# A one-core decoder layer in split float32: the first four weight chunks loaded by pairs of k tiles on one queue

## The chip, the cores and the metric

The kernel runs on one core of a Trainium2 chip. The engines are TensorE (PE, matrix products into PSUM), VectorE (DVE), ScalarE (ACT), GpSimd (POOL) and SyncE (SP, which here only issues DMAs). ACT can issue DMAs on a queue of its own. The metric is the time of one execution in microseconds (us) on the device. Three runs of the kernel before gave 439.91, 440.33 and 441.61 us; the median is 440.33.

## The reference

One decoder layer on 256 tokens of width 1024, in float32:

```
h = rmsnorm(x, norm1_g)
u = h @ w_in                      # columns: x_rnn | g_rnn | q | k | v | branch gates
ya = rg_lru(causal_dwconv(x_rnn)) * gelu(g_rnn)      # recurrent branch
yb = attention(rmsnorm(q), rmsnorm(k), v)            # 8 heads of 128, causal, one block of 256
merged = sigmoid(ga) * (ya @ w_proj_rnn) + sigmoid(gb) * (yb @ w_proj_attn)
x = x + merged @ w_out
h = rmsnorm(x, norm2_g)
x = x + (gelu(causal_dwconv(h @ w_up)) * (h @ w_gate)) @ w_down
```

The norm's division is applied after the product with w_in: the kernel multiplies x by the gains norm1_g alone, and brings in 1/rms later, on the products.

## The kernel before, in words

**Products in three parts.** To keep float32's precision at a higher rate, each operand is split into hi (rounded to the reduced type float32r) and lo (the rest). A product is three matmuls, hi by hi, hi by lo and lo by hi (`mm3`, lines 292 to 295). So each weight chunk that is loaded as `raw` goes through a cast to `hi` on ACT (or on DVE for a few) and a subtraction to `lo` on DVE (`split_part`, lines 274 to 276).

**The stream.** The weights are a list of chunks of up to 1 MB (128 partitions by 2048 elements) in the order of use, loaded on SP's queue into three `raw` buffers and split into four `hi` and three `lo` buffers. A pool of 23 half buffers (128 by 1024) holds activations. `advance(i)` makes all splits up to chunk i and keeps some loads ahead. The table `AFTER` (line 37) lists, by hand, after which quarter of which unit of PE work an item (a split `s4`, a step `stats`, `bcast`, `evac3`) is put into the program.

**Who sets the order.** The program is traced once, and a planner then decides the order of instructions on each engine: it goes by program order as priority, and by when its own table of costs says that an instruction is ready. An instruction that is ready earlier may go ahead. Inside `tc.manual_schedule` ACT and DVE keep the written order. Semaphores are put in by the framework. On the chip, each engine works through its queue in order. At most a fixed number of DMAs is under way before an issuing queue waits for an earlier one.

**The start (lines 334 to 408).** The first stage, rx, is the product of x with the first four chunks (256 columns each, 1024 rows in 8 k tiles of 128). A loop over k tiles works on all four chunks side by side in four PSUM banks (lines 706 to 710). While the first data come, nine matmuls on a tile of ones (`WARM`, line 31; lines 340 to 342) keep PE busy. Loads are cut into pieces of 1, 1, 2, 2 and 2 k tiles (`pieces`, line 345). For each piece, SP issues the load of transposed x (`xT`, line 356), and then the four chunks' pieces (line 359); for the first two pieces, chunks 2 and 3 are issued by ACT. Rows are 1 KB in those pieces and 2 KB in the rest. `pv` (line 336), all the small vectors in one tile of 170 columns, norm1_g's among them, is ACT's first load. x in token order (`xs`) comes behind the fourth piece's weights.

Then (lines 398 to 408, in the written order) each piece's x is scaled and split into `xgh` on ACT and `xgl` on DVE, and each chunk's piece is split into `hi` and `lo`; for the very first, DVE does the cast.

**Behind it.** rg takes the next four chunks. `norm1_stats` (line 416) squares `xs` on ACT, a chain of small DVE operations makes 1/rms and the diagonal tiles `dg`, and in rg's third quarter PE spreads them to all partitions (`rbcp`, line 429). Only then are rx's and rg's sums multiplied and moved out of PSUM. `gqk` (line 537) is the product of two gain columns of `pv`, used to scale k; `make_decay` on POOL also reads `pv`.

Of the kernel before, what the change touches and what calls it, by code (L numbers as in the profile page):

```python
# [8 lines left out]
F32 = mybir.dt.float32  # L9
# [6 lines left out]
P = 128  # L16
# [14 lines left out]
HALVES, SMALLS, WARM, RAWS = 23, 10, 9, 3  # L31
# [133 lines left out]
def trunk_layer(ctx: ExitStack, tc: tile.TileContext, xT, x, vec, win_fm, win_tm, wri, wpr, wpa,  # L165
# [17 lines left out]
    def f(ap):  # L183
        return ap.bitcast(F32)
# [21 lines left out]
    class Wide:  # L206


        def __init__(self, name, dt=F32):
            self.h = [half(f"{name}{i}", dt) for i in range(2)]  # L210

        def __getitem__(self, at):
            s = at[1]
            i = s.start // 1024
            assert (s.stop - 1) // 1024 == i
            return self.h[i][:, s.start - i * 1024:s.stop - i * 1024]
# [118 lines left out]
    pv = const.tile([P, V_N], F32, name="pv")  # L335
    nc.scalar.dma_start(pv, vec)
# [8 lines left out]
    pieces = [(0, 1), (1, 2), (2, 4), (4, 6), (6, 8)]  # L345
    START = 4
    for i in range(START):
        if i < 2:
            raw[i] = wp.tile([P, 2048], F32, tag="raw", name=f"raw{i}")
            split_tiles()  # L350
        else:
            raw[i], hi[i], lo[i] = Wide(f"raw{i}"), Wide(f"hi{i}", F32R), Wide(f"lo{i}", F32R)
    ptr["load"] = ptr["split"] = START
    xs = const.tile([P, 2, D], F32, name="xs")
    for a, b in pieces:
        nc.sync.dma_start(kt(xTs.half(a // 4))[:, a % 4:a % 4 + b - a, :], xT[:, a:b, :])
        for i in range(START):
            s = slice(a * 256, b * 256)
            (nc.scalar if b <= 2 and i >= 2 else nc.sync).dma_start(raw[i][:, s], stream[i][:, s])
        if a == 0:  # L360
            nc.scalar.preload_act_table(AF.Exp)
        if a == 4:
            for t in range(2):
                nc.sync.dma_start(xs[:, t, :], x[t * P:(t + 1) * P, :])
# [34 lines left out]
    with tc.manual_schedule(engines={mybir.EngineType.Activation, mybir.EngineType.DVE}):  # L399
        for a, b in pieces:  # L400
            for k in range(a, b):
                g = pv[:, V_G1 + k:V_G1 + k + 1]
                nc.scalar.activation(xgh[k], xTs[k], AF.Copy, scale=g)  # L403
                if a == 0:
                    split_part(0, slice(a * 256, b * 256), True)
                nc.vector.scalar_tensor_tensor(xgl[k], xTs[k], g, f(xgh[k]), op0=OP.mult, op1=OP.subtract)
            for i in range(a == 0, START):
                split_part(i, slice(a * 256, b * 256))
# [627 lines left out]
```

## Time and profile before

| | |
|---|---|
| median of 3 runs | 440.33 us (439.91 to 441.61) |
| profiled execution | 440.18 us, its span 438.4 us |
| PE busy | 431.3 us, 98% of the span |
| DVE, ACT, POOL busy | 325.1, 248.5, 45.8 us |
| data moved | 95.89 MB, mean 219 GB/s |

All times inside the profile count from the span's start. A row of the page or of a list of groups names the line of the kernel, the engine, the operation and what it writes and reads. In an order-of-time row, the first two numbers are the start and the time covered; square brackets give the idle time before and what ended it. "xN" is a count. PEld is the weight load into PE, which overlaps the products; PE's ends are modelled, so starts are the safer numbers. The waits list has total, times and longest, in us. Idle time of an engine that isn't the bottleneck costs nothing.

### The profile page before, as it was taken

Reading aid. Unit: us, or ns where it says so; the run is one execution under the profiler, and the core shown is the slowest. Engines: PE = TensorE matmul, PEld = TensorE weight load, DVE = VectorE, ACT = ScalarE, POOL = GpSimd, SP = SyncE. Lnnn points to the kernel's source line nnn. Section 1 sums busy time; section 2 is a strip of 40 time slices with the busy share of each in tenths; the row PEclk is TensorE's granted clock in tenths of the full one; section 3 lists DMA queues with packets and bytes.
Section 4 is the critical chain, followed back from the end, with each engine's and each line's share of the span. In section 5 each row is a group of like instructions: output and inputs, shape, how many; then the busy total and the mean of one; then the engine's idle time right before and its main releaser. Section 6 shows DMA issues by size and latency. Waiting matters only on the chain.

```text
span 438.4 us, 5841 instructions
## 1 busy us (share of the span) xinstructions
PE 431.3 (98%) x2224; PEld 368.4 (84%) x2224; DVE 325.1 (74%) x448; ACT 248.5 (57%) x294; POOL 45.8 (10%) x99
## 2 busy tenths in 40 slices
PE   8999999999899999999999999999999999999996
PEld 8999988887788888888888888888888888888985
DVE  4689869768789999765576796576776779965943
ACT  4596748682888999944232373345437257352910
POOL 2038306424240000000000000000000000000000
PEclk9999999999999999999999999999999999999999
DMA  7987652857877754554553555877995494897202
GB/s 218 387 310 256 229 193 62 240 227 233 301 253 238 230 184 151 183 171 171 191 193 96 193 191 155 280 284 275 321 309 187 148 395 190 293 340 288 86 1 96
DMA packets 30268, 95.89 MB, mean 219 GB/s; under 512 B 2848, under 2 KB 12448, under 8 KB 26144
## 3 DMA queue, kind: packets, MB, share of 16 engines
q1 hardware_dynamic: 29520, 94.91, 62.0%
q10 hardware_dynamic: 720, 0.61, 0.6%
q8 instruction: 17, 0.28, 0.3%
q14 instruction: 11, 0.09, 0.1%
HBM read 87.12 MB, written 8.39 MB: 218 GB/s over the span
## 4 chain that ended last, share of the span: by engine, by line
PE 87%; DVE 5%; POOL 3%; DMA 2%; issue 1%; ACT 1%; SPq 0%; DVEq 0%
PE acc L293 4%; PE acc L294 4%; PE acc L295 4%; PE up L293 4%; PE up L294 4%; PE gt L293 4%; PE gt L294 4%; PE up L295 4%; PE gt L295 4%; POOL rsq L388 2%; DMA raw<-in_win_fm 2%; PE rg L295 2%; PE rg L294 2%; PE rg L293 2%; PE gb L293 2%; PE v L294 2%
## 5 line engine op out<-in xcount | busy, mean ns | idle before, releaser
L276 DVE TENSOR_TENSOR lo<-raw,hi 128x2048 fp32r<-128x2048 f32 (+3 forms) x92 | 170.9, 1868 | 40.1 <-ACT hi L275 8.5
L275 ACT CAST hi<-raw 128x2048 fp32r<-128x2048 f32 (+3 forms) x88 | 137.6, 1576 | 90.7 <-PE pa L295 16.0
L294 PE MATMUL up<-lo,h2h 128*128 128x512 f32 x80 | 31.2, 391 | 0.0
L294 PE MATMUL gt<-lo,h2h 128*128 128x512 f32 x80 | 31.1, 389 | 0.0
L294 PE MATMUL acc<-lo,fah 128*128 128x512 f32 x80 | 31.1, 389 | 0.0
L293 PE MATMUL acc<-hi,fah 128*128 128x512 f32 x80 | 31.1, 389 | 0.0
L295 PE MATMUL up<-hi,h2l 128*128 128x512 f32 x80 | 31.0, 389 | 0.0
L295 PE MATMUL gt<-hi,h2l 128*128 128x512 f32 x80 | 31.0, 389 | 0.0
L293 PE MATMUL up<-hi,h2h 128*128 128x512 f32 x80 | 30.9, 392 | 0.0
L293 PE MATMUL gt<-hi,h2h 128*128 128x512 f32 x80 | 30.8, 389 | 0.0
L295 PE MATMUL acc<-hi,fal 128*128 128x512 f32 x80 | 30.5, 389 | 0.0
L853 ACT ACTIVATE fc<-fu,pv 128x256 f32<-128x256 f32 x20 | 10.4, 590 | 19.8 <-DVE fu L865 19.8
L293 PE MATMUL rx<-xgh,hi 128*128 128x256 f32 x64 | 18.3, 288 | 0.8 <-ACT xgh L403 0.8
L295 PE MATMUL rx<-xgh,lo 128*128 128x256 f32 x64 | 18.2, 284 | 0.2 <-DVE lo L276 0.2
L293 PE MATMUL rg<-xgh,hi 128*128 128x256 f32 x64 | 18.2, 284 | 0.0
L294 PE MATMUL rx<-xgl,hi 128*128 128x256 f32 x64 | 18.2, 284 | 0.0
L295 PE MATMUL rg<-xgh,lo 128*128 128x256 f32 x64 | 18.1, 283 | 0.0
L294 PE MATMUL rg<-xgl,hi 128*128 128x256 f32 x64 | 18.1, 283 | 0.0
L293 PEld LDWEIGHTS up<-hi,h2h 128*128 128x128 f32 x80 | 15.0, 188 | 3.3 <-ACT h2h L794 0.2
L293 PEld LDWEIGHTS gt<-hi,h2h 128*128 128x128 f32 x80 | 15.0, 188 | 3.2
L295 PEld LDWEIGHTS gt<-hi,h2l 128*128 128x128 f32 x80 | 15.0, 188 | 3.2
L295 PEld LDWEIGHTS acc<-hi,fal 128*128 128x128 f32 x80 | 15.0, 188 | 3.1
(251 smaller groups left out, 1078.5 us busy)
## 6 DMA issues: line engine op xcount, KB each, us to landing
raw<-in_win_tm SPq DMA_DIRECT2D x12, 1024.0 KB, 5.2
raw<-in_win_fm SPq DMA_DIRECT2D x11, 1024.0 KB, 5.7
raw<-in_wup SPq DMA_DIRECT2D x11, 1024.0 KB, 5.7
raw<-in_wgate SPq DMA_DIRECT2D x11, 1024.0 KB, 5.7
raw<-in_wdown SPq DMA_DIRECT2D x11, 1024.0 KB, 6.0
raw<-in_wpr SPq DMA_DIRECT2D x4, 1024.0 KB, 5.0
raw<-in_wpa SPq DMA_DIRECT2D x4, 1024.0 KB, 4.9
raw<-in_wout SPq DMA_DIRECT2D x4, 1024.0 KB, 4.8
```

Of the source, the lines that this page charges most:

```text
L275: (nc.vector.tensor_copy if on_dve else nc.scalar.copy)(hi[i][:, s], raw[i][:, s])
L276: nc.vector.tensor_sub(lo[i][:, s], raw[i][:, s], f(hi[i][:, s]))
L293: nc.tensor.matmul(o, ah, bh, start=start, stop=False, skip_group_check=skip)
L294: nc.tensor.matmul(o, ah, bl, start=False, stop=False, skip_group_check=skip)
L295: nc.tensor.matmul(o, al, bh, start=False, stop=stop, skip_group_check=skip)
L388: nc.gpsimd.tensor_tensor(z, y, y, op=OP.mult)
L853: nc.scalar.activation(c, u, AF.Identity, scale=w(2), bias=pv[:, V_FB + m:V_FB + m + 1])
```

## The change

- The four first chunks are no longer four tiles with pieces by k; they are pieces by pair of k tiles (a = 0 to 3) and pair of chunks (c = 0, 1), each 128 by 1024 elements, laid out as chunk, k tile, column. Pieces of a = 0 and 1 lie in `raw`, `hi` and `lo` buffers, two pieces to a buffer, those of a = 2 and 3 in half buffers. `Column` gives the matmuls the view of one chunk.
- All their loads are on SP's queue, in the order of use: x of two k tiles, then the two pieces. Every row is 2 KB. In the first pair, the piece of chunks 0 and 1 is loaded as two transfers, one a chunk.
- ACT's queue issues only `g1`, the eight columns of norm1_g. `pv`, then `xs`, are loaded on SP's queue behind all the weights of rx.
- Eight warming matmuls instead of nine.
- The splits follow the pieces: in the first, DVE casts chunk 0's two k tiles one at a time; later pieces are cast on ACT and subtracted on DVE as 128 by 1024 (the second chunk's first pair as 128 by 512).
- rx's matmuls go by pairs of k tiles: for each pair and chunk, both k tiles of the first half of its columns, then both of the second.
- `gqk` is made on POOL in two operations, so that DVE's queue doesn't hold a reader of `pv` early.
- What follows rx's first unit (`stats s4`) is queued behind the last hand-ordered instruction of ACT and of DVE (`tc.issue_after`).

```diff
-HALVES, SMALLS, WARM, RAWS = 23, 10, 9, 3
+HALVES, SMALLS, WARM, RAWS = 23, 10, 8, 3
...
-    class Wide:
+    class Column:
+        def __init__(self, pieces, i):
+            self.pieces, self.i = pieces, i
         def __getitem__(self, at):
+            k, c = divmod(at[1].start, 256)
+            return self.pieces[k // 2, self.i // 2][:, self.i % 2, k % 2, c:c + at[1].stop - at[1].start]
...
-    pv = const.tile([P, V_N], F32, name="pv")
-    nc.scalar.dma_start(pv, vec)
+    g1 = const.tile([P, KT], F32, name="g1")
+    nc.scalar.dma_start(g1, vec[:, V_G1:V_G1 + KT])
...
-    pieces = [(0, 1), (1, 2), (2, 4), (4, 6), (6, 8)]
+    def pieces(name, dt=F32):
+        p = {}
+        for a in range(2):
+            t = wp.tile([P, 2048], dt, tag=name, name=f"{name}s{a}", bufs={"raw": RAWS, "hi": 4, "lo": 3}[name])
+            for c in range(2):
+                p[a, c], p[a + 2, c] = t[:, c * 1024:(c + 1) * 1024], half(f"{name}s{a + 2}{c}", dt)
+        return {k: v.rearrange("p (c k n) -> p c k n", c=2, k=2) for k, v in p.items()}
...
-    for a, b in pieces:
+    def load_x(a, b):
         nc.sync.dma_start(kt(xTs.half(a // 4))[:, a % 4:a % 4 + b - a, :], xT[:, a:b, :])
-        for i in range(START):
-            s = slice(a * 256, b * 256)
-            (nc.scalar if b <= 2 and i >= 2 else nc.sync).dma_start(raw[i][:, s], stream[i][:, s])
...
+    def load_w(a, c, js=slice(0, 2)):
+        nc.sync.dma_start(sraw[a, c][:, js].rearrange("p c k n -> p c (k n)"),
+                          win_fm[2 * c + js.start:2 * c + js.stop, :, a * 512:(a + 1) * 512].rearrange("c p n -> p c n"))
...
+    load_x(0, 2)
+    load_w(0, 0, one)
+    nc.scalar.preload_act_table(AF.Exp)
+    load_w(0, 0, two_)
+    load_w(0, 1)
+    for a in range(1, 4):
+        load_x(2 * a, 2 * a + 2)
+        for c in range(2):
+            load_w(a, c)
+    pv = const.tile([P, V_N], F32, name="pv")
+    nc.sync.dma_start(pv, vec)
+    for t in range(2):
+        nc.sync.dma_start(xs[:, t, :], x[t * P:(t + 1) * P, :])
...
+        def split_x(k):
+            g = g1[:, k:k + 1]
+            nc.scalar.activation(xgh[k], xTs[k], AF.Copy, scale=g)
+            return lambda: nc.vector.scalar_tensor_tensor(xgl[k], xTs[k], g, f(xgh[k]), op0=OP.mult, op1=OP.subtract)
+
+        def split_w(a, c, js=slice(0, 2), ks=slice(0, 2), e=nc.scalar.copy):
+            r, h, l = sraw[a, c][:, js, ks], shi[a, c][:, js, ks], slo[a, c][:, js, ks]
+            start_end[0] = e(h, r).ins
+            return lambda: start_end.__setitem__(1, nc.vector.tensor_sub(l, r, f(h)).ins)
+
+        x = split_x(0)
+        w = split_w(0, 0, one, one, nc.vector.tensor_copy)
+        x()
+        w()
+        w = split_w(0, 0, one, two_, nc.vector.tensor_copy)
+        x = split_x(1)
+        x()
+        w()
+        split_w(0, 0, two_)()
+        split_w(0, 1)()
+        for a in range(1, 4):
+            for k in (2 * a, 2 * a + 1):
+                split_x(k)()
+            for c in range(2):
+                split_w(a, c)()
...
-    nc.vector.scalar_tensor_tensor(gqk, pv[:, V_QG:V_QG + 1], SC, pv[:, V_KG:V_KG + 1], op0=OP.mult, op1=OP.mult)
+    nc.gpsimd.tensor_scalar(gqk, pv[:, V_QG:V_QG + 1], SC, None, op0=OP.mult)
+    nc.gpsimd.tensor_tensor(gqk, gqk, pv[:, V_KG:V_KG + 1], op=OP.mult)
...
-            for k in range(KT):
+            for a in range(KT // 2):
                 for n in range(START):
-                    fm_mm(rx_ps[n], n, xgh, xgl, (k,), True)
+                    fm_mm(rx_ps[n], n, xgh, xgl, (2 * a, 2 * a + 1), True)
...
-            for n in AFTER.get(f"{name}.{q}", "").split():
-                advance(int(n[1:])) if n[1:].isdigit() and n[0] == "s" else item[n]()
+            with tc.issue_after(start_end[0]) if name == "rx0" else nullcontext(), \
+                    tc.issue_after(start_end[1]) if name == "rx0" else nullcontext():
+                for n in AFTER.get(f"{name}.{q}", "").split():
+                    advance(int(n[1:])) if n[1:].isdigit() and n[0] == "s" else item[n]()
```

31 lines of the change are left out of this document (5 added, 26 removed).

## The prediction

> **What bounds the kernel now.** I read the page first, then the waits of TensorE (PE), then busy time by stage, then the first microseconds in order of time.
>
> ```profile
> span 438.4 us, 5841 instructions
> PE 431.3 (98%) x2224; PEld 368.4 (84%) x2224; DVE 325.1 (74%) x448; ACT 248.5 (57%) x294; POOL 45.8 (10%) x99
> PE 87%; DVE 5%; POOL 3%; DMA 2%; issue 1%; ACT 1%; SPq 0%; DVEq 0%
> ```
>
> PE is busy for 98% of the span and holds 87% of the chain that ended last. An edit helps only where PE stands still. The list of what PE waited for is short:
>
> ```profile
> PE v L293 <- ACT hi L275: 0.9, 1, 0.9
> PE rx L293 <- ACT xgh L403: 0.8, 1, 0.8
> PE v L294 <- DVE lo L276: 0.5, 1, 0.5
> PE rx L295 <- DVE lo L276: 0.2, 1, 0.2
> ```
>
> Two of these lie in rx, the stage the change rewrites; the two in v come far behind it and the change does not name them. The stage view gives the size of the start. Its columns are window, length, then busy time and count for PE, weight loads, DVE, ACT, POOL, then the granted clock, DMA share and GB/s.
>
> ```profile
> 0.00:5.42 5.42, 3.62 (x18) 3.43 (x19) 1.09 (x5) 1.84 (x3) 2.24 (x12) 1.00 0.64 189
> 5.42:29.52 24.10, 23.88 (x192) 23.36 (x193) 16.35 (x35) 16.66 (x34) 0.48 (x2) 1.00 0.96 340
> 29.52:53.00 23.48, 23.48 (x198) 23.48 (x197) 20.15 (x28) 15.74 (x13) 15.91 (x34) 1.00 0.71 260
> 34.01 0.45 PE rbcp L429 x4
> ```
>
> rx starts at 5.42 and rg at 29.52. The rg stage has 192 products of the same shape and the rbcp matmuls in 23.48 us: (23.48 - 0.45) / 192 = 0.12 us each. So rx, also 192, needs 23.03 us and took 24.10: it lost 1.07 us to late operands. With the wait for the first operands, all that the change can win directly is 5.42 + 1.07 = 6.5 us less whatever the first load and splits still need. Now the first load:
>
> ```profile
> 0.72 0.37 SPq L356 DMA_DIRECT2D xT<-in_xT  x1
> 1.16 0.93 ACTq L359 DMA_DIRECT2D raw<-in_win_fm  x2
> 2.12 1.28 ACT L361 ACT_TABLE_LOAD   x1 [2.12 <-issue]
> 3.82 0.99 ACTq L359 DMA_DIRECT2D raw<-in_win_fm  x2
> 4.48 0.32 DVE L275 CAST hi<-raw 128x256 fp32r<-128x256 f32 x1 [0.31 <-DMA raw<-in_win_fm]
> 4.83 0.42 DVE L276 TENSOR_TENSOR lo<-raw,hi 128x256 fp32r<-128x256 f32 x1
> 4.86 0.51 ACT L403 ACTIVATE xgh<-xT,pv 128x256 fp32r<-128x256 f32 x1 [1.46 <-DMA raw<-in_win_fm]
> 5.40 0.48 DVE L406 SCALAR_TENSOR_TENSOR xgl<-xT,pv,xgh 128x256 fp32r<-128x256 f32 x1
> 5.42 0.69 PE L293 MATMUL rx<-xgh,hi 128*128 128x256 f32 x2 [0.76 <-ACT xgh L403]
> 5.80 1.09 DVE L276 TENSOR_TENSOR lo<-raw,hi 128x256 fp32r<-128x256 f32 x3
> ```
>
> The weights landed in time for DVE's cast at 4.48, but xgh, the scaled x, began only at 4.86: ACT was issuing two more weight DMAs from 3.82 to 4.81. PE's first product waited for xgh until 5.42.
>
> **The change part by part.**
>
> *ACT's queue.* Four weight DMAs and pv leave it; a load of g1 (4 KB in rows of 32 B) stays. ACT's 3.82 to 4.81 is gone, so xgh is bound by x and g1. Landing times from the tile views, x first, weights second, and pv's from the DMA view:
>
> ```profile
> DMA to landing us min/median/max: 3.1/5.3/8.5
> DMA to landing us min/median/max: 3.3/5.5/8.5
> pv<-in_vec ACTq DMA_DIRECT2D x1, 85.0 KB, 3.3
> ```
>
> The smallest, 3.1 us for the first 128 KB of x issued at 0.72, gives 3.8; x now brings 256 KB first. g1's price does not show: its bounds are 0 (inside x's 3.1 us) and pv's row count at pv's place, which took 3.3 us for the same 128 partitions and so landed at 4.0. I take 3.9 for both, xgh of the first tile from 3.9 to 4.4, and nothing on the path since the weights land later. The Trainium skill, "DMA: Bandwidth & Descriptors", section "Rules for kernel authors", speaks against such a load: it says to coalesce, since a transfer under 64 KB is mostly overhead. By that rule g1 would land no sooner than pv did; at 4.0 xgh would end at 4.5 and the sum would not move by 0.1 us. No row of before has a load as small.
>
> *The first weights.* Data moved in the first microseconds:
>
> ```profile
> 1.00:2.00 1.00, 0.96 (x4) 0.97 (x5) 0.00 (x0) 0.00 (x0) 0.96 (x4) 1.00 0.10 25
> 2.00:3.00 1.00, 1.00 (x7) 1.00 (x6) 0.00 (x0) 0.88 (x1) 0.10 (x1) 1.00 0.86 165
> 3.00:4.00 1.00, 1.00 (x7) 1.00 (x7) 0.00 (x0) 0.40 (x1) 0.00 (x0) 1.00 0.98 333
> 4.00:5.00 1.00, 0.66 (x6) 0.47 (x5) 0.65 (x3) 0.14 (x1) 0.71 (x3) 1.00 1.09 374
> ```
>
> That is 25 + 165 = 190 KB by 3.0 and 523 KB by 4.0. The first weights (landed just before 4.48) needed 128 KB of x, their own 128 KB, and an equal share of the other queue beside them, 512 KB in all, which had moved by about 3.97: half a microsecond lies between moving and landing. After the change the first weights need 256 KB of x, their own 256 KB and g1, again about 516 KB. So their landing T stays at 4.45. Bounds: 3.9 if the slow 2.00 to 3.00 was pv's doing and 374 GB/s hold from 2.1; 4.9 if the larger first load comes a whole 128 KB share plus one issue (0.45) later.
>
> *The first splits.* DVE now does, for two k tiles in turn, hi, xgl, lo. By durations that is 2 x (0.32 + 0.48 + 0.42) = 2.44 us; starts are closer than durations (xgl at 5.40, the next at 5.80: 0.40, and three lo in 1.09: 0.34), which gives about 0.25 + 0.40 + 0.34 + 0.25 + 0.40 + 0.42 = 2.06. I take 2.1 with the step to PE, since the closer starts are measured. fm_mm takes both k tiles before its second half, so PE's first product starts near T + 0.35 = 4.8, and its sixth, the last that needs a fresh lo, at 4.45 + 2.1 = 6.55. From there 186 remain and rg starts after them, the sixth included at 187 x 0.12 = 22.4 us later: 28.97.
>
> *Whether the rest of rx keeps up.* Prices of the larger splits:
>
> ```profile
> 25.74 1.03 ACT L275 CAST hi<-raw 128x1024 fp32r<-128x1024 f32 x1
> 16.64 0.69 DVE L276 TENSOR_TENSOR lo<-raw,hi 128x512 fp32r<-128x512 f32 x1 [0.30 <-ACT hi L275]
> 26.80 1.23 DVE L276 TENSOR_TENSOR lo<-raw,hi 128x1024 fp32r<-128x1024 f32 x1 [1.29 <-ACT hi L275]
> 10.75 0.88 DVE L406 SCALAR_TENSOR_TENSOR xgl<-xT,pv,xgh 128x256 fp32r<-128x256 f32 x2
> ```
>
> At 374 GB/s from 4.0 and half a microsecond to land, 768 KB (second chunk) is there at 5.2, 1280 KB (third and fourth) at 6.5. DVE's lo of the second chunk runs 6.45 to 7.15; PE wants it at 7.5. Its lo of the next two runs to 8.75; PE wants it at 8.95, so 0.2 us to spare. A later pair of k tiles costs DVE 0.88 + 2 x 1.23 = 3.34 us and PE 48 x 0.12 = 5.76, so the spare grows by 2.4 us a pair, and data for a pair (1.25 MB, 3.4 us) also outruns PE. The 1.07 us of old stalls go; what is late next is DVE's first lo, already in the sum.
>
> *SP's queue.* It takes over four weight pieces, but pairs make it fewer issues: 25 transfers of x and weights before, four of them on ACT, against 13, at about 0.45 us each (two took 0.93). With 374 GB/s a 512 KB piece takes 1.4 us, so issue hides behind the data. pv and xs move behind the weights: 5.1 MB and 6.1 MB have moved by about 16.3 and 19 us.
>
> ```profile
> 31.41 0.48 DVE L423 TENSOR_SCALAR dg<-ident,rs 128x128 f32<-128x128 f32 x2
> ```
>
> dg was ready at 31.9 and PE wanted it at 34.0; xs landing at 19.5 leaves 12 us to that point for two Squares and some small operations, so dg comes no later. pv's users (decay on POOL, whose result is wanted only in the recurrence, and conv, which comes behind the evacuation of rx) wait for other work until long after that. gqk on POOL instead of DVE: two small operations, used only when k is turned for the scores, nothing. Raw buffers come free after the first pairs, so chunks 5 and 6 can load earlier: more cover, no gain, since rg had no PE wait.
>
> *Eight warming matmuls.* PE ends its warming 0.1 to 0.2 us sooner and then waits for weights: nothing, unless the clock depends on it (below).
>
> *Sum.* rg starts at 28.97 instead of 29.52: 0.55 us. Its own range: T at 3.9 gives 1.1 us, T at 4.9 gives 0.1, and DVE without overlap takes 0.35 from either. Everything behind is PE work and moves with it. The profiled execution took 440.18 us, 1.78 around its span, and the median of the runs is 440.33, 0.15 above; 440.33 - 0.55 = 439.8. The likeliest case's own range is 439.2 to 440.6.
>
> **The rivals.**
>
> *A. The later order turns against it.* The planner sets the order of DVE, ACT and PE from its own times, and the hand table was laid against the old start. With loads, stats and splits early, a full lo may be put ahead of something PE needs; the place to look is the start of v, where PE already waits 0.9 + 0.5 us for a hi and then a lo. One more hi and lo in that series costs
>
> ```profile
> 29.20 1.91 ACT L275 CAST hi<-raw 128x2048 fp32r<-128x2048 f32 x1 [0.33 <-DMA raw<-in_win_fm]
> 34.01 2.29 DVE L276 TENSOR_TENSOR lo<-raw,hi 128x2048 fp32r<-128x2048 f32 x1
> ```
>
> 1.91 + 2.29 = 4.2 us: 440.33 - 0.55 + 4.2 = 444.0. It decides once the new wait passes 2.75 us. For it: v's wait shows so little cover there. Against: once rx's buffers are recycled, loads and splits are released by PE, which moves as a block.
>
> *B. The same, the other way.* v's wait of 1.4 us goes and T is 3.9: 440.33 - 1.1 - 1.4 = 437.8. Only together do they pass 2.2 us.
>
> *C. No gain.* T at 4.9, or DVE slower between small pieces: 440.3. For it: T is the term with the widest bounds.
>
> *D. The clock.* Warming matmuls started 0.21 us apart, then 0.11:
>
> ```profile
> 1.03 3.62 PE L342 MATMUL warm<-ones 128*128 128x128 f32 x18 [1.03 <-DVE ones L338]
> 2.27 0.63 PE L342 MATMUL warm<-ones 128*128 128x128 f32 x2
> 2.48 0.64 PE L342 MATMUL warm<-ones 128*128 128x128 f32 x2
> 3.94 0.39 PE L342 MATMUL warm<-ones 128*128 128x128 f32 x2
> 4.05 0.50 PE L342 MATMUL warm<-ones 128*128 128x128 f32 x3
> ```
>
> PE doubled its rate near 3.8, 2.8 us after its first matmul at 1.03, although the granted clock reads 1.00 throughout. If eight matmuls and then six spread products don't hold it, dense work runs at half rate for another 2.8 us, losing 1.4: 441.2. Against: the doubling came with 0.8 us of warming left. The Trainium skill, "TensorE: Matmul & The Clock Gate", section "Part 1: The HAM clock gate", says the clock opens after a busy window of some 3.4 us that runs free of the kernel's start; by that figure the loss is an estimated 1.7 us. The doubling agrees with it in kind, and no run here shows another phase of the window.
>
> **How the numbers follow.** The forecast 0.35, C 0.20, D 0.08, A 0.25, B 0.12. Within 0.5% (2.2 us, about what a measurement of this kernel can tell from no change) lie the first three: 0.63. Faster is B, slower is A. The range 438.2 to 444.0 leaves out B and the far end of A; it is wide above because A's price is.
>
> **What would show it.** xgh starts near 3.9 and DVE's first hi near 4.5; PE's first product near 4.8 and its sixth near 6.6; no PE wait after that in rx; rg starts near 29.0; the wait in v is still about 1.4 us. Wrong if T lies beyond 4.9, if rx products start 0.24 us apart, if PE waits for dg, or if a wait of over 2.75 us stands anywhere behind rx.

## The result, and the profile after

The changed kernel takes 442.20 us, the median of 20 runs (440.73 to 444.26), against 440.32 us for the kernel before (20 runs, 439.91 to 441.95). The ratio is 1.0045, with a 95% interval of 1.0031 to 1.0059. It is slower by 1.9 us, where 0.5 us of gain was forecast. The profiled execution took 442.12 us with a span of 440.0.

The page of the changed kernel, its totals and its chain by engine, answers to the first rows of the prediction:

```profile
span 440.0 us, 5798 instructions
PE 433.0 (98%) x2222; PEld 370.2 (84%) x2222; DVE 323.6 (74%) x438; ACT 247.4 (56%) x283; POOL 45.1 (10%) x101
PE 86%; DVE 6%; POOL 3%; DMA 2%; issue 1%; ACT 0%; SPq 0%; DVEq 0%
```

PE is busy 1.7 us longer, with two matmuls fewer. Longer busy time for less work points at PE's rate; which of rate and wait sets the end is read further down. The waits of PE:

```profile
PE v L291 <- ACT hi L273: 0.9, 1, 0.9
PE rx L293 <- DVE los L427: 0.6, 1, 0.6
PE v L292 <- DVE lo L274: 0.5, 1, 0.5
PE rx L291 <- DVE his L426: 0.4, 1, 0.4
```

The two waits in v are the same 0.9 and 0.5 us as before. The wait for xgh has gone, as forecast, but rx now waits for a los. The stage view (window, length, busy time and count for PE, weight loads, DVE, ACT, POOL, then the granted clock, DMA share and GB/s) is cut at rx's first product, at the product where its rate doubles, and at rg's first:

```profile
0.00:5.23 5.23, 3.78 (x16) 3.52 (x17) 0.60 (x3) 2.19 (x3) 1.54 (x9) 1.00 0.55 164
5.23:9.44 4.21, 4.21 (x18) 4.04 (x19) 2.12 (x6) 1.16 (x2) 0.00 (x0) 1.00 0.92 301
9.44:31.27 21.83, 21.26 (x177) 21.05 (x176) 16.73 (x27) 17.19 (x22) 2.58 (x5) 1.00 0.96 381
31.27:54.70 23.43, 23.43 (x198) 23.43 (x197) 16.82 (x22) 12.38 (x12) 13.96 (x35) 1.00 0.57 208
```

rx starts 0.19 us earlier than before (5.23 against 5.42), and rg 1.75 us later (31.27 against 29.52). Between the two rx needs 23.03 us and took 26.04: it lost 3.0 us where it had lost 1.07. From rg on everything is shifted by the same amount (v starts at 118.44, before at 116.70). The loss lies in rx's first six microseconds, and the order of time shows two things there:

```profile
4.18 0.91 ACT L421 ACTIVATE xgh<-xT,g 128x256 fp32r<-128x256 f32 x2 [1.74 <-DMA g<-in_vec]
4.79 0.29 DVE L426 CAST his<-raws 128x256 fp32r<-128x256 f32 x1 [3.81 <-DMA raws<-in_win_fm]
5.23 0.55 PE L291 MATMUL rx<-xgh,his 128*128 128x256 f32 x1 [0.41 <-DVE his L426]
...
7.52 0.41 PE L291 MATMUL rx<-xgh,his 128*128 128x256 f32 x1
...
7.73 0.41 PE L292 MATMUL rx<-xgl,his 128*128 128x256 f32 x1
...
8.90 1.05 ACT L426 CAST his<-raws 128x1024 fp32r<-128x1024 f32 x1 [2.45 <-DMA raws<-in_win_fm]
...
9.57 0.28 PE L291 MATMUL rx<-xgh,his 128*128 128x256 f32 x1
...
9.69 0.28 PE L292 MATMUL rx<-xgl,his 128*128 128x256 f32 x1
...
9.98 1.23 DVE L427 TENSOR_TENSOR los<-raws,his 128x1024 fp32r<-128x1024 f32 x1 [2.63 <-ACT his L426]
...
10.41 0.28 PE L292 MATMUL rx<-xgl,his 128*128 128x256 f32 x1
...
11.26 0.38 PE L293 MATMUL rx<-xgh,los 128*128 128x256 f32 x1 [0.57 <-DVE los L427]
```

**The rate.** Products start 0.21 us apart until 9.44 (7.52, 7.73), and then 0.12 (9.57, 9.69). Before, the rate had doubled at 3.9. The seventeen products from 5.23 to 9.44 take 4.2 us; at 0.12 they would be 2.0. Part of that is not the rate: the first six wait for DVE's splits, as forecast. At 9.44 PE is 1.45 us behind the forecast (sixth product at 6.55, then 12 x 0.12: 7.99), 0.43 of it from the later first product and about 1.0 from the rate. The column of the granted clock reads 1.00 all the while, so the spacing of starts has to be read.

**The late piece.** The 512 KB with the first two k tiles of chunks 2 and 3 are there only at 8.90, where ACT's cast had waited 2.45 us for them. Cast and subtraction follow one another on the whole piece, 1.05 + 1.23 us, so the los is ready at 11.2. PE's 27th product waits for it, and starts at 11.26. The 166 that remain take 166 x 0.12 = 19.9 us: 31.2. So in this execution the late piece sets rx's end; with a full rate PE would only have waited longer for it. Three other profiles with this split, in two of which the clock had opened before the first product, bear that out below.

Data moved in the same microseconds, by the stage view:

```profile
4.00:5.00 1.00, 0.82 (x4) 0.52 (x3) 0.21 (x1) 0.82 (x2) 0.00 (x0) 1.00 0.92 279
5.00:6.00 1.00, 0.77 (x3) 0.70 (x3) 1.00 (x5) 0.26 (x2) 0.00 (x0) 1.00 0.95 326
6.00:7.00 1.00, 1.00 (x5) 0.93 (x5) 1.00 (x4) 0.45 (x1) 0.00 (x0) 1.00 0.88 254
7.00:8.00 1.00, 1.00 (x7) 1.00 (x6) 0.35 (x1) 0.00 (x0) 0.00 (x0) 1.00 0.75 209
8.00:9.00 1.00, 1.00 (x6) 1.00 (x6) 0.00 (x0) 0.10 (x1) 0.00 (x0) 1.00 1.00 367
```

The rate falls to 209 GB/s where the prediction had 374 hold. That is the smaller part of the delay. By 7.00 us 197 x 7 = 1.38 MB had moved:

```profile
0.00:7.00 7.00, 5.55 (x22) 5.12 (x23) 2.37 (x8) 2.81 (x4) 1.54 (x9) 1.00 0.65 197
```

The loads up to and with this piece are 1284 KB, or 1.31 MB, and had been moved, by the mean rate, near 6.8; with the prediction's half microsecond the piece would land at 7.3 instead of 6.5. A load is there when the last of its shares is. The trace keeps the sixteen counts by which this load's semaphore rises, a step for each share: fourteen came between 6.41 and 7.30 us, and the last two at 8.77 and 8.88. These two shares cost 1.6 us, twice what the lower rate did.

In the DMA view the seven pieces of 512 KB, most of which queue behind others, take a median of 8.7 us from issue to landing; this one, issued at 2.08, took 6.8:

```profile
raws<-in_win_fm SPq DMA_DIRECT2D x7, 512.0 KB, 8.7
g<-in_vec ACTq DMA_DIRECT2D x1, 4.0 KB, 3.4
```

The same weakness was in the kernel before. Its last early piece, the second k tile of chunk 3, was cast late too:

```profile
9.90 0.41 ACT L275 CAST hi<-raw 128x256 fp32r<-128x256 f32 x1 [1.72 <-DMA raw<-in_win_fm]
```

But there only 6 of the first 48 products needed that 128 KB piece, and PE had enough others; now 24 of the first 48 hang on one piece of 512 KB.

**Outside the span.** All 20 runs spend 2.11 to 2.21 us outside the span; the 108 runs of before that stood beside the experiments, 1.73 to 1.85. That is 0.35 us of the 1.9, in a place the prediction took as fixed.

### The profile page after: what moved, and what is told of

Same layout as the page of the kernel before. It is cut to its first block, busy times and chain, and to the rows that moved or that the text cites. A ratio compares the mean times of both kernels' runs of the same rounds, so it can differ in the third digit from the quotient of the medians.

```text
span 440.0 us, 5798 instructions
## 1 busy us (share of the span) xinstructions
PE 433.0 (98%) x2222; PEld 370.2 (84%) x2222; DVE 323.6 (74%) x438; ACT 247.4 (56%) x283; POOL 45.1 (10%) x101
## 4 chain that ended last, share of the span: by engine, by line
PE 86%; DVE 6%; POOL 3%; DMA 2%; issue 1%; ACT 0%; SPq 0%; DVEq 0%
PE acc L291 4%; PE acc L292 4%; PE acc L293 4%; PE up L291 4%; PE up L292 4%; PE gt L292 4%; PE up L293 4%; PE gt L291 4%; PE gt L293 4%; POOL rsq L405 2%; DVE lo L274 2%; PE rg L291 2%; PE rg L293 2%; PE rg L292 2%; PE gb L291 2%; PE v L292 2%
## 5 line engine op out<-in xcount | busy, mean ns | idle before, releaser
L274 DVE TENSOR_TENSOR lo<-raw,hi 128x2048 fp32r<-128x2048 f32 (+1 forms) x72 | 159.8, 2224 | 40.1 <-ACT hi L273 11.2
L273 ACT CAST hi<-raw 128x2048 fp32r<-128x2048 f32 (+1 forms) x69 | 127.8, 1862 | 94.5 <-PE pa L293 16.0
L292 PE MATMUL up<-lo,h2h 128*128 128x512 f32 x80 | 31.2, 390 | 0.0
L291 PE MATMUL rx<-xgh,his 128*128 128x256 f32 x64 | 19.0, 300 | 0.4 <-DVE his L426 0.4
L293 PE MATMUL rx<-xgh,los 128*128 128x256 f32 x64 | 18.8, 297 | 0.6 <-DVE los L427 0.6
L292 PE MATMUL rx<-xgl,his 128*128 128x256 f32 x64 | 18.8, 297 | 0.0
L293 PEld LDWEIGHTS up<-hi,h2l 128*128 128x128 f32 x80 | 15.0, 188 | 3.1
```

The costliest lines, as they stand in the source:

```text
L273: (nc.vector.tensor_copy if on_dve else nc.scalar.copy)(hi[i][:, s], raw[i][:, s])
L274: nc.vector.tensor_sub(lo[i][:, s], raw[i][:, s], f(hi[i][:, s]))
L291: nc.tensor.matmul(o, ah, bh, start=start, stop=False, skip_group_check=skip)
L292: nc.tensor.matmul(o, ah, bl, start=False, stop=False, skip_group_check=skip)
L293: nc.tensor.matmul(o, al, bh, start=False, stop=stop, skip_group_check=skip)
```

## The experiments

The theory that I took up is two losses in rx's start: PE's rate, and the late coarse piece. The rivals: the rate alone (the piece is hidden behind it), the piece alone, the later order behind rx (the prediction's rival A), or one of the small parts (g1, the number of warming matmuls). Every ratio is against runs of the kernel before on the same chip.

### The kernel again, and fourteen warming matmuls

The changed kernel unaltered:

> The changed kernel unaltered, for its spread and for a second profile on the same chip as the runs beside it. Clock theory (the array's clock opens later or closes again while the first products are spread out, by a phase that differs from run to run): two groups of runs, one with a mean granted clock of 1.0 near 441.5 us and one with 0.996 near 443.3 us. Load theory (the piece of chunks 2 and 3 of the first pair lands near 8.9 us and sets when rx can go on): in the profile the lo of that piece ends near 11.2 us and the rg stage starts no sooner than 166 products of 0.12 us later, near 31.2 us, whatever the clock. Together: median near 442.2 us.

Measured 442.41 us (441.47 to 442.73), ratio 1.0031 [1.0019, 1.0043]. The loss is there again; the two groups of runs that were expected are not (one run of seven has a mean clock of 0.996). In its profile the piece was cast at 9.52, the rate doubled at 9.4 and rg started at 31.89.

```diff
-HALVES, SMALLS, WARM, RAWS = 23, 10, 8, 3
+HALVES, SMALLS, WARM, RAWS = 23, 10, 14, 3
```

> The changed kernel with fourteen warming matmuls instead of eight, so that they reach to 5.8 to 7 us and the clock has opened before rx begins. Clock theory: no run of the 0.996 group is left, the median falls by about 1 us to 441.2 us and the spread shrinks to that of before (2 us). Load theory: the products wait for the lo of chunks 2 and 3 near 11.2 us anyway, 24 products of 0.12 us fit between 7 and 10 us, and the median stays at 442.2 us. Neither: over 443 us, because PE starts rx 2 us later.

Measured 441.57 us (440.44 to 443.92), 1.0017 [1.0001, 1.0034]. The order of time:

```profile
6.56 0.28 PE L292 MATMUL rx<-xgl,his 128*128 128x256 f32 x1
...
8.30 1.05 ACT L426 CAST his<-raws 128x1024 fp32r<-128x1024 f32 x1 [1.46 <-DMA raws<-in_win_fm]
...
9.62 0.28 PE L292 MATMUL rx<-xgl,his 128*128 128x256 f32 x1
...
10.66 0.38 PE L293 MATMUL rx<-xgh,los 128*128 128x256 f32 x1 [0.76 <-DVE los L427]
```

Products run at 0.12 us from the start, though they start a microsecond later. The median is 0.8 us below the repeat's, but the two intervals overlap, and two of the twelve runs still have a clock of 0.996. The wait for the los stays and is longer (products start at 9.62 and then at 10.66): a faster PE runs into the piece sooner.

The profiles say more than the medians. rg starts 22.37 us after ACT's cast of the piece in the changed kernel (31.27 after 8.90), in the repeat (31.89 after 9.52), here (30.67 after 8.30), and in the kernel with pv in two transfers further down (30.92 after 8.55). The clock opened at 9.45, 9.4, 5.6 and 5.1 us. So in all four the piece alone sets rx's end, and the slow rate is hidden behind it; this profile is shorter because the piece landed earlier. What the warming does in runs without a profile is not seen.

### The piece in two halves: as transfers, as splits

Four kernels cut the piece of chunks 2 and 3 in two: first both its transfer and its split, the same with fourteen warming matmuls, then each alone.

```diff
-    load_w(0, 1)
+    load_w(0, 1, one)
+    load_w(0, 1, two_)
...
-        split_w(0, 1)()
+        split_w(0, 1, one)()
+        split_w(0, 1, two_)()
```

> The changed kernel with the first pair's piece of chunks 2 and 3 loaded as two transfers of 256 KB and split one chunk at a time, as chunks 0 and 1 are. Load theory: chunk 2 lands 0.7 us or more ahead of 8.85 and its lo no longer waits for chunk 3, so the 0.73 us stall after the 26th product goes and the median falls by 0.7 us to 441.5 us. Clock theory: two groups of runs remain, 443 and 441 us, and the median moves by less than 0.3 us.

> Fourteen warming matmuls and the piece of chunks 2 and 3 as two transfers and two splits. If the slow clock and the late piece are the two halves of the loss and each was only hidden behind the other, rg starts at 29.9 or before and the median is 440.5 to 440.9. If the loads alone set the end of rx whatever the clock does, the wait only moves to the next pair, rg starts at 30.7 as with fourteen matmuls alone, and the median is 441.2 to 441.6, less 0.3 if the time outside the span goes with the number of transfers.

> The piece of chunks 2 and 3 as two transfers, its cast and subtraction still in one. The kernel with two transfers and two splits had 1.82 to 1.91 us outside the span, the changed kernel 2.10 to 2.21. If the number of transfers sets that time, 1.85 here; if the number of splits, 2.15. The span: the split waits for the later of two transfers, so no shorter than the changed kernel's, 440 to 441.

> One transfer, two splits. Outside the span 2.15 if transfers count, 1.85 if splits do. The span: chunk 2's lo is ready 0.4 to 0.5 us sooner (cast 0.62 and subtraction 0.69 instead of 1.05 and 1.23), so if that lo sets the end of rx, rg starts 0.4 to 0.6 earlier than in the changed kernel; if the clock sets it alone, no difference.

| | median us (range) | ratio | outside the span, us |
|---|---|---|---|
| both | 442.51 (442.26 to 442.75) | 1.0038 [1.0026, 1.0050] | 1.82 to 1.91 |
| both, fourteen warming | 442.35 (441.92 to 444.23) | 1.0048 [1.0028, 1.0068] | 1.82 to 1.90 |
| two transfers | 443.11 (442.88 to 445.27) | 1.0068 [1.0043, 1.0093] | 2.11 to 2.20 |
| two splits | 441.13 (440.27 to 444.23) | 1.0021 [1.0001, 1.0040] | 1.74 to 1.86 |

None of the medians expected for the first two came out. Cutting the split helps, cutting the transfer does not: with two transfers the second half was cast at 9.76 in the first kernel, no sooner than the whole, and its wait moved to the next pair of k tiles, which came a transfer later:

```profile
12.22 1.05 ACT L427 CAST his<-raws 128x1024 fp32r<-128x1024 f32 x1 [0.44 <-DMA raws<-in_win_fm]
...
14.58 0.38 PE L293 MATMUL rx<-xgh,los 128*128 128x256 f32 x1 [0.76 <-DVE los L428]
```

With two splits alone, half the piece is ready nearly 1 us sooner after its landing (9.18 + 1.29 / 2 is 1.3 us after the cast's start at 8.53; for the whole piece it was 2.3), and no wait for a los is left in this profile, in which PE also ran at half rate from 7.6 to 11.0 us:

```profile
8.53 1.14 ACT L426 CAST his<-raws 128x512 fp32r<-128x512 f32 x2 [2.00 <-DMA raws<-in_win_fm]
...
9.18 1.29 DVE L427 TENSOR_TENSOR los<-raws,his 128x512 fp32r<-128x512 f32 x2 [1.38 <-ACT his L426]
```

The last column of the table settles the 0.35 us outside the span: it goes with one more cast and one more subtraction, and not with the transfers. A transfer more in a place where nothing waits says the same:

```diff
-    nc.sync.dma_start(pv, vec)
+    nc.sync.dma_start(pv[:, :V_G1], vec[:, :V_G1])
+    nc.sync.dma_start(pv[:, V_G1:], vec[:, V_G1:])
```

> The small vectors, behind the weights, as two transfers: one transfer more in the kernel, in a place where nothing waits. If the number of transfers sets the time outside the span, 1.85 and a median 0.3 below the changed kernel's (441.9); if it is the place or the shape of the split transfer, 2.15 and no difference (442.2).

Measured 441.77 us (441.49 to 443.82), 1.0035 [1.0019, 1.0050], and 2.10 to 2.21 us outside the span in all ten runs. Its start is the changed kernel's. In its profile the clock opened at 5.1 us, before the first product at 5.74, and rg still starts at 30.92, 1.4 us later than before, behind the late piece:

```profile
8.55 1.05 ACT L427 CAST his<-raws 128x1024 fp32r<-128x1024 f32 x1 [1.95 <-DMA raws<-in_win_fm]
```

Why one instruction more on ACT and DVE makes the rest shorter is open; the span's records do not reach there.

In the profile of the kernel with two transfers alone the granted clock shows what a slow rate is, in a form that the changed kernel's profile hides:

```profile
5.00:7.00 2.00, 1.41 (x6) 1.03 (x7) 1.85 (x6) 1.16 (x3) 0.00 (x0) 1.00 0.95 241
7.00:8.00 1.00, 1.00 (x6) 0.96 (x7) 0.70 (x2) 0.00 (x0) 0.00 (x0) 0.69 0.70 168
...
10.00:11.00 1.00, 1.00 (x6) 0.78 (x5) 0.10 (x1) 0.98 (x2) 0.00 (x0) 0.61 1.02 389
```

Here the clock was open for the first products and was then halved. A mean of 0.69 from 7 to 8 puts that at 7.4, and 0.61 from 10 to 11 puts the end at 10.8, 3.4 us later. Even that is hidden: the piece was cast at 9.82, and rg started at 32.20, 22.38 us later. In the changed kernel's profile the clock had not been open yet, and such a stretch isn't recorded.

### The kernel before, with one part of the change each

One warming matmul fewer (9 to 8); g1 alone on ACT's queue, with pv behind the weights and gqk on POOL; and ACT's four weight pieces on SP's queue:

```diff
-    pv = const.tile([P, V_N], F32, name="pv")
-    nc.scalar.dma_start(pv, vec)
+    g1 = const.tile([P, KT], F32, name="g1")
+    nc.scalar.dma_start(g1, vec[:, V_G1:V_G1 + KT])
...
-            (nc.scalar if b <= 2 and i >= 2 else nc.sync).dma_start(raw[i][:, s], stream[i][:, s])
+            nc.sync.dma_start(raw[i][:, s], stream[i][:, s])
```

> The kernel before with eight warming matmuls, the only edit. Clock theory in its simplest form (the ninth matmul is what opens the clock in time): slower by about 1 us, 441.3 us, with runs of a clock of 0.996 as in the changed kernel. Load theory: 440.3 us, unchanged, since its pieces land as before. If the clock hangs on how spread the first products are and not on the ninth matmul, also unchanged.

> The kernel before with one part of the change alone: ACT's first load is norm1's eight columns, the other small vectors come behind the weights of rx on SP's queue, and gqk is made on POOL. If the 680 byte rows of those vectors slowed the first microseconds, the first product starts up to 0.5 us sooner than 5.4 to 5.7 us and the time falls by as much, 440.1 us. If the first product is bound by ACT issuing two weight loads until 4.8 us, no change, 440.6 us. Clock and load theories say nothing against either: no run over 441.5 us beyond those the kernel before has.

> The kernel before with one part of the change alone: the four pieces that ACT issued go to SP's queue, so all weights are on one queue in their old shape. If one queue as such delays the first pairs (load theory in its queue form), chunks 2 and 3 of the first k tile are split later than 6.6 us, PE waits in rx for over 2 us in all, and the time rises by 1 us or more, to 441.6 us. If the delay hangs on the shape of the pieces (512 KB, two chunks and two k tiles at once), it stays within 0.5 us of 440.6.

| | median us (range) | ratio |
|---|---|---|
| eight warming | 441.20 (440.19 to 442.79) | 1.0009 [0.9997, 1.0021] |
| g1 alone | 439.99 (439.54 to 441.62) | 0.9991 [0.9978, 1.0005] |
| one queue | 441.01 (440.77 to 442.52) | 1.0019 [1.0010, 1.0028] |

Eight warming matmuls are no clear loss on the old start, and g1 alone costs nothing: it is the best of all these kernels, though not clear of no change. One queue costs 0.65 us, between the two values expected. It makes the first product earlier (4.80), as the prediction argued for ACT's queue, and the last early piece later, which PE then waits for:

```profile
PE rx L293 <- ACT hi L275: 1.5, 2, 1.1
10.73 0.41 ACT L275 CAST hi<-raw 128x256 fp32r<-128x256 f32 x1 [2.81 <-DMA raw<-in_win_fm]
```

### Why the piece lands late

Three theories. SP issues the later pairs' loads, whose data take the DMA engines before the slowest of them has finished this piece; then holding those loads back lets it land at about 7.5. Or the pattern of the pieces in memory is slow; then pieces that lie contiguous there, 4 KB to a partition, land sooner. Or one queue moves too little; then a second queue brings the piece earlier.

```diff
+    nc.gpsimd.tensor_copy(xTs[2][:, 0:1], sraw[0, 0][:, 1, 0, 0:1])
     for a in range(1, 4):
```

> The changed kernel with the loads of the second to fourth pair held back until chunk 1's first piece has landed (near 5.8 us), by a one-column copy on POOL into the place that the next load writes. Skew theory (the 16 engines run ahead into the next pair's loads while the slowest still moves the piece of chunks 2 and 3, and slow it): that piece lands at 7.5 us instead of 8.3 to 9.5, its lo ends near 10 us, and the later pairs, issued some 3 us later, land just before they are wanted: 441.5 us. If the slowest engine is slow by itself, that piece lands at 8.9 us as before and the held loads come late: over 443 us.

The copied column is overwritten by the load that it holds back. Measured 444.17 us (443.22 to 445.40), 1.0089 [1.0065, 1.0113]. The piece was cast at 8.40, and the x of the next pair came far too late:

```profile
1.15 2.56 SPq L364 DMA_DIRECT2D raws<-in_win_fm  x5
...
8.40 1.04 ACT L427 CAST his<-raws 128x1024 fp32r<-128x1024 f32 x1 [1.97 <-DMA raws<-in_win_fm]
...
12.47 0.91 ACT L422 ACTIVATE xgh<-xT,g 128x256 fp32r<-128x256 f32 x2 [3.03 <-DMA xT<-in_xT]
```

But the added copy does not do what it was meant to. The column belongs to the x of the second pair, so that load alone waits for the copy, until 6.19, and with it what SP issues behind it. The two weight pieces of the second pair are the fourth and fifth of the loads that SP issued from 1.15 to 3.71, without a pause: they followed the piece of chunks 2 and 3 sooner than in the changed kernel, where the second x comes between. So the data that the theory blames were there as before, and it stays untested. Fifteen of the piece's sixteen shares had landed by 7.26, and the last at 8.38.

```diff
-                          win_fm[2 * c + js.start:2 * c + js.stop, :, a * 512:(a + 1) * 512].rearrange("c p n -> p c n"))
+                          first[2 * a + c, :, js.start * 512:js.stop * 512])
```

> The changed kernel with the first four chunks laid out so that each piece is contiguous: 4 KB a partition in one run instead of two rows of 2 KB that lie 1 MB apart, within rows 8 KB apart; nothing else. Layout theory (the first pass over four chunks touches 4 MB in rows far apart, and that is why packets take 100 to 150 ns instead of 84 until 8 us): the piece of chunks 2 and 3 lands at 7 us, its lo ends near 9.5, and the time falls by 1 us to 441.4 us. If it is the start itself that is slow, whatever the layout: landing at 8.3 to 9.5 us and 442.4 us.

Measured 442.59 us (442.37 to 443.47), 1.0055 [1.0038, 1.0072]. The cast of the piece comes at 8.08, with its shares spread evenly from 6.33 to 8.06, but the first weights are cast 1.4 us later than in the changed kernel's profile:

```profile
6.15 0.29 DVE L426 CAST his<-raws 128x256 fp32r<-128x256 f32 x1 [5.17 <-DMA raws<-in_first]
```

The layout theory falls, as far as one profile and four runs tell: another order in memory moves the wait to the front.

```diff
-    load_w(0, 1)
+    load_w(0, 1, q=nc.scalar)
```

> The changed kernel with one edit: the first pair's piece of chunks 2 and 3 is issued by ACT, behind its table load, so that two queues feed the transfer engines at the start as before. Queue theory (two queues at once move more than one, because one can go on while a packet of the other is held up): the piece lands near 7.5 us instead of 8.3 to 9.5, its lo ends near 10, and the median falls by 0.7 us to 441.6 us; the clock still opens late in most runs. If the piece is late because the engines are slow at the start whatever feeds them: landing after 8.3 us, 442.3 us.

Measured 443.97 us (443.20 to 444.66), 1.0080 [1.0067, 1.0092]. ACT issued the piece at 1.19, beside the table load and not behind it as expected, and its 512 KB shared the DMA engines with what is needed first:

```profile
1.19 0.42 ACTq L364 DMA_DIRECT2D raws<-in_win_fm  x1
...
5.99 0.29 DVE L426 CAST his<-raws 128x256 fp32r<-128x256 f32 x1 [5.01 <-DMA raws<-in_win_fm]
```

The piece's last share landed at 7.20, 1.7 us sooner than in the changed kernel and sooner than the 7.5 expected of a second queue; ACT came to it at 8.35, right behind the second chunk's cast. But the first weights came 1.2 us later. The Trainium skill, "DMA: Bandwidth & Descriptors", section "Issuing engines are not separate DMA queues", has SP's and ACT's transfers run on the same DMA engines; this run agrees. Why those engines move so little from 6 to 8 us (254 and 209 GB/s in the changed kernel, 223 and 167 before) and about 400 after 9, and why one or two shares of the piece come so far behind the rest, stays open; that the loads behind them take the engines is possible and not tested.

### The rate, taken together with the piece

The last kernel with eleven warming matmuls; the same with two transfers and two splits for ACT's piece; and the kernel before with g1 alone and eleven:

> The same with eleven warming matmuls, so that PE stays busy until 5 to 5.7 us. Clock and queue theories together: the clock has opened by 6.7 us in every phase of its window, the lo of chunks 2 and 3 ends near 10 us, the rg stage starts near 30 us and the median is near 440.6 us, as before. If only the clock counted, 441.5 us, as with fourteen matmuls; if only the queue, 441.6 us.

> The same again with that piece as two transfers and two splits, one a chunk. If the size of the piece still holds PE up (its cast and subtraction take 2.3 us in series for 1024 columns), the wait in rx for its lo shrinks by up to 1 us, to 440 us; if the loads are the limit, no change from the run above.

> The kernel before with norm1's columns alone on ACT's queue, the other small vectors behind, and eleven warming matmuls instead of nine. Clock theory: the two more matmuls fill the gap before the first product, the late phases (the runs above 441 us) go, and the median falls to 439.9 us with a spread of 1 us. If the gap doesn't matter: 440.0 us with the same spread up to 441.6 us. Against: over 440.5 us, where the matmuls run past the moment the first operands are ready.

Measured 443.64 us (442.00 to 446.06), 1.0083 [1.0055, 1.0110]; 443.35 (441.56 to 445.05), 1.0063 [1.0046, 1.0081]; and 440.71 (439.81 to 442.73), 1.0011 [0.9999, 1.0023]. The first two are some 3 us above what was expected of them. In their profiles the early loads come at nearly the same times (first cast 6.12 and 6.30), and rg starts at 33.67 and 31.14. Most of the 2.5 us between them is the rate; one row of each:

```profile
9.92 0.41 PE L292 MATMUL rx<-xgl,his 128*128 128x256 f32 x1
```

```profile
9.31 0.28 PE L293 MATMUL rx<-xgh,los 128*128 128x256 f32 x1
```

In the first, products kept 0.21 us apart until 13.99, in spite of the eleven warming matmuls; here the rate does set the end: rg starts 25.1 us after the cast of the piece at 8.54. The third adds nothing to g1 alone, and lies above the 440.5 that was named against it. In both profiles of that shape the clock opened only at 6.6 to 7.1, and rg still started at 29.8 and 29.5: with small pieces the old start gets by.

Last, all three terms at once: two splits on one transfer, with eleven and with fourteen warming matmuls.

> Two splits on one transfer, and eleven warming matmuls. If the three terms (time outside the span 0.35, the late piece's split, the slow clock 0.8) add up to the whole loss, the median is 440.3 to 440.7, no different from the kernel before, and the first 48 products stand 0.12 us apart. If eleven don't reach the opening of the clock or the first two terms already hold all that can be won, 441.0 to 441.4 as with eight.

> The same with fourteen. The clock opens before the first product in nearly every run, but the warming ends at about 6.4 us instead of 5.7, later than the first operands at 5.2 to 5.6: 440.6 to 441.0, with fewer long runs than with eleven. If the clock has no part in it, 441.3 or more, for the later start alone.

Measured 440.92 us (440.34 to 442.08), 1.0010 [1.0000, 1.0019], and 441.00 us (440.42 to 442.16), 1.0014 [1.0005, 1.0023]. The first lies between the two ranges expected, the second at the end of its own. By the ratios, 0.0035 of the 0.0045, some 1.5 us of the 1.9 to 2.0, are gone. About half a microsecond stays. In the profile with eleven, the piece was cast at 9.60, late as ever, and PE still waits:

```profile
PE rx L291 <- ACT his L426: 0.7, 1, 0.7
PE rx L293 <- DVE los L427: 0.5, 2, 0.3
```

**How often the clock closes.** The runs of one kernel spread over more than 3 us, and the mean granted clock of a run goes with that. Of the changed kernel's 20 runs, 11 show 0.996 and took 443.31 us in the mean; the other 9 took 441.55. A mean of 0.996 is one stretch of 3.4 us at half rate (0.004 x 440 = 1.76 us, with 0.996 itself rounded), and 443.31 - 441.55 = 1.76. All six profiles with that mean hold exactly one such stretch. Of the 108 runs of the kernel before, 5 show it (442.19 against 440.49). The unaltered start was measured twice more (the repeat, and pv in two): 3 of 17, so the share of 11 in 20 is not firm. With two splits it is 3 in 10, with eleven or fourteen warming matmuls besides, 1 in 11 and 1 in 12; and there the runs without it took 440.90 and 440.96, no less than the 440.92 with two splits and eight. So the split also shortens runs without a closing. That more warming makes the closings rarer is suggested by these counts, not shown. Four profiles show the half clock between 7 and 13 us (two transfers, two splits, the contiguous pieces, the second queue), one from 16.9 to 20.3 (the held load), one from 123.2 to 126.6 (ACT's piece with eleven warming). They belong to altered kernels; no trace of the changed kernel itself caught one, so where its eleven lie is not known.

## Why the prediction was wrong, step by step

**Right.**
- All of the effect inside the span lies in rx; v's wait is still 0.9 + 0.5 us, and rg, k and all behind move rigidly. Rival A, which carried most of the chance of a loss, did not happen, nor did B.
- ACT's queue: ACT issued nothing late. xgh started at 4.18, not 3.9, because g1 took 3.4 us to land (3.0 with g1 alone on the old start, 4.7 with the contiguous pieces). It cost nothing, since DVE's first cast came at 4.79.
- DVE's first splits took 2.0 us (4.79 to about 6.75), as summed from the closer starts (2.06).
- pv, xs and gqk: no one waits for them.
- T was 4.77 instead of 4.45, within its bounds of 3.9 to 4.9; 0.3 us of the gain. The repeat had 5.2, beyond them.

**Wrong: "768 KB (second chunk) is there at 5.2, 1280 KB (third and fourth) at 6.5".** This is the step that failed. The piece of chunks 2 and 3 was cast at 8.90, and at 8.3 to 9.6 in the seven profiles that load it so (the changed kernel, its repeat, fourteen warming, two splits with eight, eleven and fourteen, pv in two). The step took a load for landed when its bytes, at the mean rate of all the engines, have moved. In these seven profiles the fourteenth of the piece's sixteen shares came at 7.3 to 7.8 us, and the last at 8.3 to 9.6; the wait is for the last. The lower rate is the lesser error (7.3 instead of 6.5). The step used that of the one best microsecond (374 GB/s, from 4.00 to 5.00), though the same view of before goes on like this, and though the prediction's own rows named landing times of up to 8.5 us:

```profile
6.00:7.00 1.00, 1.00 (x10) 1.00 (x10) 1.00 (x4) 1.00 (x3) 0.00 (x0) 1.00 0.88 223
7.00:8.00 1.00, 1.00 (x11) 1.00 (x10) 0.72 (x3) 0.53 (x2) 0.00 (x0) 1.00 0.92 167
```

It also took "PE wants it at 8.95, so 0.2 us to spare" for safety, where half a microsecond of error in a landing ends it (by its own spacing the 27th product, the first to need that lo, is due at 9.07, which changes little). The step priced the coarser split rightly (1.05 and 1.23 us) and overlooked that 24 of 48 products now depend on one of them. In the four profiles with this split that alone sets rx's end, 22.37 us after the cast; in the changed kernel's, 2.3 us behind the forecast 28.97. Cutting the split in two, in runs whose mean clock is above 0.996, won 0.6 to 1.2 us (440.92 against 441.55, 441.81 and 442.16 in three measurements of the unaltered start), 0.35 of it outside the span.

**Wrong in part: "Eight warming matmuls ... nothing", and rival D at 0.08.** The mechanism was described: "If eight matmuls and then six spread products don't hold it". It came: in the profile the clock opened at 9.45, products stood 0.21 us apart, and at that moment PE was about 1.0 us behind the forecast for it (the prediction's own sign of this was "if rx products start 0.24 us apart"). But the end of rx did not move by it, since the piece came later still, and D's 441.2 is not how the time came about. Apart from that, a recorded closing goes with 1.76 us more in the 20 runs, and no trace shows how. The evidence against D was one execution: the doubling at 3.8 with 0.8 us of warming left. With another phase the same warming ends before it. The Trainium skill, "TensorE: Matmul & The Clock Gate", section "Part 1: The HAM clock gate", says just that, a window of some 3.4 us that does not start with the kernel; the runs agree, in the half-clock stretch of 3.4 us, and in the moments at which the rate doubled in different profiles: 3.9, 5.6, 6.4, 9.4 and 14.0 us. The prediction named the rule and then let one phase decide.

**Wrong: the time around the span.** "440.18 us, 1.78 around its span" was carried over; it became 2.15. No row of before could have shown it.

**How they add up.** The changed kernel's profiled execution took 1.94 us more than that of before: 0.35 outside the span, and 1.6 inside it, where rx ends with the piece. The piece and the rate are not a sum: they stand side by side, and rx ends with the later one. The medians fit that only roughly: fourteen warming matmuls alone gave 0.8 us, two splits alone about 1.1 (0.35 of it outside the span), both together about 1.5 by the ratios, and their intervals overlap. What share of the changed kernel's median comes from closings of the clock is open. That 442.20 lies inside the stated range of 438.2 to 444.0 is luck: the range is wide above for rival A's price, and A did not happen. Where the last half microsecond comes from is seen (the piece still lands at 9 to 9.6) but not cured: neither another layout, nor a second queue, nor smaller transfers did it, and the loads behind the piece were never held back.

## What to carry to other kernels

In the first ten microseconds, time each load by landing rows of loads as large and as early, not by bytes over a mean rate, since the last share counts, and count how many products can run before the last byte: fine pieces late in the order hide what one coarse piece shows. Where the first products come in a trickle, ask in which state the clock will find them, and read the spacing of starts, since the clock's column may not show it. Where two delays stand side by side, look in several profiles which of them the end follows before either is given a share of the loss.

## What was not expected of the hardware

- The granted clock's column reads 1.00 until the clock first opens, even at half rate: 0.21 us between products at 7.52 and 7.73, 0.12 at 9.57 and 9.69.
- An open clock was closed while PE was working through spread products: in the kernel with two transfers PE was busy 1.41 of the 2 us from 5 to 7 and all of 7 to 8, and the clock was halved at 7.4. It was also seen behind stalls: with the x of the second pair held back from 16.9 on, after PE had been busy for 1.54 of the 3 us from 13 to 16, and with ACT's piece and eleven warming matmuls once behind v's wait, which all these kernels have.

```profile
122.00:150.00 28.00, 27.46 (x122) 22.44 (x121) 23.84 (x50) 23.66 (x33) 4.85 (x13) 0.94 0.73 233
```

- The time outside the span takes one of two values, 1.73 to 1.91 or 2.10 to 2.21 us, and one more cast and subtraction switched the changed kernel from the one to the other.
- Of the sixteen shares of the 512 KB load, the last landed 0.7 to 1.9 us behind the fourteenth in all seven profiles of that piece.
- A load of 4 KB took 3.0, 3.4 or 4.7 us to land, with other loads beside it each time; 85 KB had taken 3.3.
